# Arithmetic on SBUF moved from Pool to VectorE and TensorE, and a 64x64 product moved from the norms to the third feed-forward pair

## The chip, the cores and the metric

The kernel runs on one core of one Trainium2 chip. The metric is the device time of one launch in microseconds (us); smaller is better. The engines of a core go by the names of the profile: PE is TensorE's matmul, PEld its weight load, DVE is VectorE, ACT is ScalarE, POOL is GpSimd (Pool in the text), SP is SyncE, which issues the loads of the weights.

## What is computed

Two layers of a decoder trunk on 256 tokens of width 1024, in float32. The reference, cut to its skeleton:

```python
h = x
for i in range(2):
    xn = rmsnorm(h, norm_mix[i])
    u_nsa, u_hgrn, u_ret, u_rwkv = split(xn @ w_in[i])
    outs = nsa(u_nsa), hgrn2(u_hgrn), retention(u_ret), rwkv7(u_rwkv)      # 256 wide each
    merged = sum(sigmoid(xn @ w_gate[i, m] + b_gate[i, m]) * (outs[m] @ w_branch[i, m]) for m in range(4))
    h = h + merged @ w_out[i]
    hn = rmsnorm(h, norm_ffn[i])
    h = h + (silu(hn @ w_ffn_gate[i]) * (hn @ w_ffn_up[i])) @ w_ffn_down[i]   # 2816 wide
    hp = rmsnorm(h, norm_ple[i])
    h = h + sigmoid(hp @ w_ple_gate[i]) * (p[i] @ w_ple_proj[i])
return rmsnorm(h, norm_final)
```

rmsnorm divides each token by the root of the mean of its 1024 squares (plus 1e-6) and multiplies by a gain per feature.

## The kernel before

Activations lie feature-major, [128 features, 8 chunks, 256 tokens], so that weights are TensorE's stationary operand and tokens the moving one. A GEMM keeps float32 accuracy by splitting both operands in a high and a low part. `w_load` (lines 197 to 213) takes a weight tile of 128x1024: SP's queue loads it (512 KB) into `wr`, ACT copies it into the high part `wh` (L211), and a subtraction gives the low part `wl` (L212); there are 4 buffers of `wr` and 3 each of `wh` and `wl`. `mm3` (L226 to L228) then issues three matmuls per block of 128x128, wl with xh, wh with xl, wh with xh, each over 256 columns: 24 matmuls per tile. `gemm_pair` (L261 to L263) is the same for two output chunks, with the last contraction chunks put last where these are produced late.

The subtraction goes to DVE or to Pool: Pool takes every fourth tile (`wcount % 4 == 3`) while `shared` is set, which is from the gates of the mixer m=3 on to the next layer, and at the last stage of a layer a list, `lo_plan`, names the engine tile by tile. Pool also adds the merged branches (L1255), multiplies in the feed-forward stage (L1343), adds up squares for the norms (L336, L340, L345) and does one residual add per layer (L1365, by `adders`).

A layer goes through these stages: input projection and the four mixers; the gates and branches of the mixers, m = 2, 1, 3, 0; the projection w_pp of p; w_out with a residual; 11 pairs of feed-forward chunks (two gate tiles and two up tiles each); w_fd with a residual; and the PLE stage, which is four pairs of w_pg, a tanh, a product and the add to h (L1362 to L1365). The order of the instructions on each engine is made by a scheduler from priorities; `issue_after` pins one instruction behind another.

A norm is spread: `h_done` is called for each finished chunk of h, makes its high and low parts (L315, L316), squares it (L327, L331) and adds squares up. `h_stat` (L348 to L372) sums the squares over features by products with a column of 1/1024 (L354, 128x1, two per accumulated tile), takes the root in ten small DVE operations (L285 to L299), and spreads it over the partitions with two matmuls (L359). The GEMMs that follow don't wait for it: their results are multiplied by it afterwards. Where `steady` is set (at the first norm, behind both w_out, and between the layers), a product of 64x64 with two columns, whose result nobody reads, follows the spreading:

```python
with self.tc.issue_after(bcast.ins):
    q = slice(0, 64)
    self.nc.tensor.matmul(bc[q, T:T + 2], self.ident[q, q], self.ident[q, :2], start=True, stop=True,
                          tile_position=(0, 0), skip_group_check=True)
```

This product (L365) is called the quarter product here. Four of them run, one for each norm that `steady` names.

## Time and profile before

| quantity | value |
|---|---|
| time, median of 3 runs | 1037.78 us (1036.01 to 1038.59) |
| time of the profiled execution | 1037.06 us |
| span of the profiled execution | 1035.3 us |
| mean granted clock of TensorE | 0.994 |
| PE busy | 1016.1 us, 98% |
| DVE busy | 735.6 us, 71% |
| ACT busy | 542.1 us, 52% |
| POOL busy | 241.9 us, 23% |

The span is what the trace covers; 1.8 us of the profiled execution's own time lie around it. The profile gives TensorE's granted clock in shares of its full speed of 2.4 GHz; 0.5 is its lower level, 1.2 GHz. The shares are averages over stages. A wait in the trace is put down to the semaphore that came last. Matmuls overlap, so the pace of a stream of matmuls is read from their starts: each lasts 0.28 us, and the next starts long before it ends.

### The profile page before, as it was taken

How to read it: one execution, taken by the hardware profiler on the slowest of the kernel's cores; microseconds unless marked ns; L12 is line 12 of the kernel's file. 1: busy time of each engine (PE TensorE's matmuls, PEld its weight loads, DVE VectorE, ACT ScalarE, POOL GpSimd, SP SyncE). 2: the span in 40 equal slices, each digit the busy share in tenths (PEclk: the TensorE clock that was granted, in tenths of full speed). 3: DMA queues.
4: the chain of work that ended last, by engine and by line, in shares of the span. 5: the costliest groups of instructions: out<-in, count | busy, mean ns of one | idle time of the engine just before them, and what ended most of it. 6: DMA issues, size and time to landing. Idle time of an engine off the chain costs nothing.

```text
span 1035.3 us, 22817 instructions
## 1 busy us (share of the span) xinstructions
PE 1016.1 (98%) x9528; PEld 975.6 (94%) x9528; DVE 735.6 (71%) x1216; ACT 542.1 (52%) x863; POOL 241.9 (23%) x154
## 2 busy tenths in 40 slices
PE   9999999999999999999899999999999999999996
PEld 8999988899999999999898999988999999999995
DVE  6899968766676767554877999577556767765556
ACT  5644555554664555454545545556546555454444
POOL 0100000054442233233410000000544333242322
PEclk9999999999999999999999999999999999999998
DMA  8565233255665666666544553333656665666651
GB/s 292 183 201 157 90 104 109 76 163 175 208 198 167 204 200 185 194 187 206 167 156 128 182 165 103 103 103 102 173 185 183 193 189 179 207 191 192 182 185 53
DMA packets 50503, 171.33 MB, mean 165 GB/s; under 512 B 5856, under 2 KB 6624, under 8 KB 50272
## 3 DMA queue, kind: packets, MB, share of 16 engines
q1 hardware_dynamic: 50112, 169.76, 53.4%
q8 instruction: 75, 1.23, 0.5%
q14 instruction: 28, 0.23, 0.1%
q10 hardware_dynamic: 288, 0.11, 0.0%
HBM read 168.80 MB, written 1.05 MB: 164 GB/s over the span
## 4 chain that ended last, share of the span: by engine, by line
PE 86%; DVE 9%; ACT 2%; issue 1%; DMA 1%; POOL 1%; DVEq 0%; ACTq 0%; POOLq 0%
PE mm L226 21%; PE mm L227 21%; PE mm L228 21%; PE pB L141 6%; PE pA L141 5%; DVE wl L212 2%; PE pA L226 2%; PE pA L227 2%; PE pA L228 2%; PE pA L261 1%; PE pA L262 1%; PE pA L263 1%; ACT wh L211 1%; DVE T L1364 1%; PE mm L438 1%
## 5 line engine op out<-in xcount | busy, mean ns | idle before, releaser
L211 ACT ACTIVATE wh<-wr 128x1024 fp32r<-128x1024 f32 (+3 forms) x314 | 325.4, 1040 | 333.8 <-PE mm L228 221.2
L212 DVE TENSOR_TENSOR wl<-wr,wh 128x1024 fp32r<-128x1024 f32 (+3 forms) x259 | 325.2, 1257 | 131.7 <-ACT wh L211 130.6
L226 PE MATMUL mm<-xh,wl 128*128 128x256 f32 x1472 | 412.6, 280 | 1.4 <-POOL wl L212 1.4
L228 PE MATMUL mm<-xh,wh 128*128 128x256 f32 x1472 | 411.1, 279 | 0.0
L227 PE MATMUL mm<-xl,wh 128*128 128x256 f32 x1472 | 411.0, 279 | 0.0
L226 PEld LDWEIGHTS mm<-xh,wl 128*128 128x128 f32 x1472 | 276.7, 188 | 5.3 <-POOL wl L212 1.8
L227 PEld LDWEIGHTS mm<-xl,wh 128*128 128x128 f32 x1472 | 277.1, 188 | 3.0 <-issue 1.4
L228 PEld LDWEIGHTS mm<-xh,wh 128*128 128x128 f32 x1472 | 276.7, 188 | 2.5 <-issue 1.1
L212 POOL TENSOR_TENSOR wl<-wr,wh 128x1024 fp32r<-128x1024 f32 (+1 forms) x55 | 130.3, 2370 | 260.8 <-ACT wh L211 260.8
L226 PE MATMUL mm<-A,wl 128*128 128x256 f32 x332 | 91.6, 276 | 0.0
L227 PE MATMUL mm<-A,wh 128*128 128x256 f32 x332 | 91.6, 276 | 0.0
L228 PE MATMUL mm<-A,wh 128*128 128x256 f32 x332 | 91.6, 276 | 0.0
L1343 POOL TENSOR_TENSOR B<-B,B 128x512 f32<-128x512 f32 x22 | 28.4, 1292 | 145.7 <-DVE B L1341 139.4
L226 PEld LDWEIGHTS mm<-A,wl 128*128 128x128 f32 x332 | 62.3, 188 | 0.0
L227 PEld LDWEIGHTS mm<-A,wh 128*128 128x128 f32 x332 | 62.3, 188 | 0.0
L228 PEld LDWEIGHTS mm<-A,wh 128*128 128x128 f32 x332 | 62.3, 188 | 0.0
L382 DVE TENSOR_TENSOR A<-B,A 128x512 fp32r<-128x512 f32 x18 | 36.8, 2042 | 33.2 <-ACT A L381 33.2
L141 PE MATMUL pA<-A,A 64*64 64x64 f32 (+3 forms) x1008 | 49.7, 223 | 1.2 <-DVE A L644 1.2
L141 PEld LDWEIGHTS pA<-A,A 64*64 64x64 f32 (+3 forms) x1008 | 41.6, 135 | 9.0 <-DVE A L644 1.6
L1255 POOL TENSOR_TENSOR M<-M,T 128x512 f32<-128x512 f32 x24 | 43.4, 1843 | 9.9 <-DVE T L1254 9.9
L226 PE MATMUL mm<-Y,wl 128*128 128x256 f32 x160 | 44.8, 280 | 0.0
L227 PE MATMUL mm<-Y,wh 128*128 128x256 f32 x160 | 44.5, 278 | 0.0
(393 smaller groups left out, 1741.9 us busy)
## 6 DMA issues: line engine op xcount, KB each, us to landing
wr<-in_w_gate_dram SPq DMA_DIRECT2D x64, 512.0 KB, 3.7
wr<-in_w_fm_dram SPq DMA_DIRECT2D x46, 512.0 KB, 3.7
wr<-in_w_fg_dram SPq DMA_DIRECT2D x44, 512.0 KB, 4.6
wr<-in_w_fu_dram SPq DMA_DIRECT2D x44, 512.0 KB, 3.7
wr<-in_w_fd_dram SPq DMA_DIRECT2D x32, 512.0 KB, 4.2
wr<-in_w_branch_dram SPq DMA_DIRECT2D x16, 512.0 KB, 4.2
wr<-in_w_out_dram SPq DMA_DIRECT2D x16, 512.0 KB, 3.8
wr<-in_w_pg_dram SPq DMA_DIRECT2D x16, 512.0 KB, 3.9
```

The costliest lines, as they stand in the source:

```text
L141: f(*args, **kw)
L211: nc.scalar.activation(hi[:, s], raw[:, s], AF.Copy)
L212: e.tensor_sub(lo[:, s], raw[:, s], hi[:, s])
L226: mm(out, wlo, xhi, start=start, stop=False)
L227: mm(out, whi, xlo, start=False, stop=False)
L228: mm(out, whi, xhi, start=False, stop=stop)
L261: mm(ps[:, c], lo, xs[k][0], start=c == 0 and k == 0, stop=False, skip_group_check=True)
L262: mm(ps[:, c], hi, xs[k][1], start=False, stop=False, skip_group_check=True)
L263: mm(ps[:, c], hi, xs[k][0], start=False, stop=k == n - 1, skip_group_check=True)
L382: self.nc.vector.tensor_sub(lo, src, hi)
L1255: self.nc.gpsimd.tensor_add(merged[p], merged[p], ths[p])
L1343: G.tensor_mul(up, th, up)
```

## The change

All of Pool's arithmetic on SBUF goes to DVE: the subtraction of 55 weight tiles, 22 products of the feed-forward stage, 24 adds of merged branches, the adds of squares and two residual adds. Pool keeps memsets, conversions and small copies. At the PLE stage `h_done` is called with `plain`: there, only the squares of the first two chunk pairs are added (on DVE), and the others go to TensorE as they are, so that six tiles instead of two (layer 0) or four (layer 1) are multiplied with the column of 1/1024. The quarter products behind the norms are gone; in each layer one stands before the gate product of the third feed-forward pair, pinned behind the matmul that was issued last.

```diff
--- before.py
+++ after.py
@@ -201,15 +201,11 @@
         raw = self.wp.tile([P, 1024], F32, tag="wr", name=f"wr{self.n}", bufs=WRAW)
         hi = self.wp.tile([P, 1024], F32R, tag="wh", name=f"wh{self.n}", bufs=WSPL)
         lo = self.wp.tile([P, 1024], F32R, tag="wl", name=f"wl{self.n}", bufs=WSPL)
-        self.wcount += 1
-        e = nc.gpsimd if self.wcount % 4 == 3 and self.shared else nc.vector
-        if self.lo_plan:
-            e = nc.gpsimd if self.lo_plan.pop(0) == "P" else nc.vector
         for i in range(0, n, n // parts):
             s = slice(i, i + n // parts)
             self.last_load = nc.sync.dma_start(raw[:, s], src[:, s])
             nc.scalar.activation(hi[:, s], raw[:, s], AF.Copy)
-            e.tensor_sub(lo[:, s], raw[:, s], hi[:, s])
+            nc.vector.tensor_sub(lo[:, s], raw[:, s], hi[:, s])
         return hi, lo
 
     def w_tiles(self, src, parts=1):
@@ -225,7 +221,14 @@
         mm = self.nc.tensor.matmul
         mm(out, wlo, xhi, start=start, stop=False)
         mm(out, whi, xlo, start=False, stop=False)
-        mm(out, whi, xhi, start=False, stop=stop)
+        self.last_mm = mm(out, whi, xhi, start=False, stop=stop)
+
+    def quarter(self, ps):
+
+        q = slice(0, 64)
+        with self.tc.issue_after(self.last_mm.ins):
+            self.nc.tensor.matmul(ps[q, 0, :2], self.ident[q, q], self.ident[q, :2], start=True, stop=True,
+                                  tile_position=(0, 0), skip_group_check=True)
 
     def mm2(self, out, w, x, start, stop):
 
@@ -300,7 +303,7 @@
         return y
 
 
-    def h_done(self, ch, gcol, tag=None, first=False, part=None):
+    def h_done(self, ch, gcol, tag=None, first=False, part=None, plain=False):
 
         nc = self.nc
         p, c = divmod(ch, 2)
@@ -329,9 +332,16 @@
                 return
         else:
             nc.scalar.activation(sq, self.h[:, ch - 1:ch + 1], AF.Square)
-        add = nc.vector.tensor_add if first else nc.gpsimd.tensor_add
+        add = nc.vector.tensor_add
         if p == 0:
             self.acc = sq
+        elif plain and p > 1:
+
+            if p == 2:
+                self.accs = [self.acc[:, 0], self.acc[:, 1]]
+            if p == 2 or c == 1:
+                self.accs += [sq[:, 0], sq[:, 1]]
+            return
         elif p < 3 - (gcol is None):
             add(self.acc, self.acc, sq)
         if p == 2:
@@ -345,7 +355,7 @@
                 add(sq[:, 0], sq[:, 0], sq[:, 1])
                 self.accs.pop()
 
-    def h_stat(self, last=False, steady=False):
+    def h_stat(self, last=False):
         nc = self.nc
         ps = self.ps([P, 512], "pB")
         n = len(self.accs)
@@ -356,14 +366,8 @@
         self.rt = self.rsqrt(ps[:, 0:2], 2, 1.0, EPS)
         bc = self.ps([P, 512], "pB")
         for tc_ in range(2):
-            bcast = nc.tensor.matmul(bc[:, tc_ * P:(tc_ + 1) * P], self.rt[:, tc_:tc_ + 1].to_broadcast([P, P]), self.ident,
+            nc.tensor.matmul(bc[:, tc_ * P:(tc_ + 1) * P], self.rt[:, tc_:tc_ + 1].to_broadcast([P, P]), self.ident,
                              start=True, stop=True)
-        if steady:
-
-            with self.tc.issue_after(bcast.ins):
-                q = slice(0, 64)
-                self.nc.tensor.matmul(bc[q, T:T + 2], self.ident[q, q], self.ident[q, :2], start=True, stop=True,
-                                      tile_position=(0, 0), skip_group_check=True)
         self.rstd_ps = bc[:, None, :T].to_broadcast([P, 2, T])
         if last:
             return
...
@@ -1191,14 +1195,9 @@
         self.omlb = [om[:, 2 * l:2 * l + 2] for l in range(L)]
 
     def body(self):
-        self.wcount = 0
-
-        self.shared = False
         self.tc.cur_priority += Front.AHEAD
         self.xp = [None] * 4
         self.stream = "B"
-
-        self.lo_plan = list("VVVVV")
         self.setup()
         for p in range(4):
             for c in range(2):
@@ -1206,7 +1205,7 @@
             if p == 2:
                 self.ahead.append(self.w_tiles([self.ins["w_fm"][0, 7]], 2))
                 self.nc.sync.dma_start(self.h[:, 6:8], self.ins["x"][:, 6:8])
-        self.h_stat(steady=True)
+        self.h_stat()
         for l in range(L):
             self.layer(l)
 
@@ -1252,18 +1251,17 @@
                     V.scalar_tensor_tensor(merged[p], ths[p], 1.0, ps, op0=OP.add, op1=OP.mult)
                 else:
                     V.scalar_tensor_tensor(ths[p], ths[p], 1.0, ps, op0=OP.add, op1=OP.mult)
-                    self.nc.gpsimd.tensor_add(merged[p], merged[p], ths[p])
+                    V.tensor_add(merged[p], merged[p], ths[p])
 
     def layer(self, l):
         nc = self.nc
-        V, G = nc.vector, nc.gpsimd
+        V = nc.vector
         ins = self.ins
         v = lambda col: self.vec[l][:, col:col + 1]
         vh = lambda col: self.vech[l][:, col:col + 1]
         self.merged = [None] * 4
         lane = self.lane
         self.lanes = dict.fromkeys("GAB", self.tc.cur_priority)
-        self.shared = False
         with lane("G"):
             ums = self.rwkv_in(l)
         with lane("A", "G"):
@@ -1302,7 +1300,6 @@
         with lane("G"):
             self.tc.cur_priority += (200, 100)[l]
             for m, y in ((2, y2), (1, y1), (3, y3), (0, y0)):
-                self.shared = m in (3, 0)
                 self.branch(l, m, self.gates(l, m), y)
         self.tc.cur_priority = max(self.lanes.values())
 
@@ -1330,6 +1327,8 @@
         xs = []
         for p in range(NF // 2):
             pg = self.ps([P, 2, T], "mm" if p else "pA")
+            if p == 2:
+                self.quarter(pg)
             self.gemm_pair(pg, [[ins["w_fg"][l, 2 * p + c]] for c in range(2)], self.xs(), 0 if p else 2)
             pu = self.ps([P, 2, T], "mm" if p else "pA")
             self.gemm_pair(pu, [[ins["w_fu"][l, 2 * p + c]] for c in range(2)], self.xs())
@@ -1340,15 +1339,13 @@
             up = self.g([P, 2, T])
             V.tensor_mul(up, pu, self.rstd_b)
             V.scalar_tensor_tensor(th, th, 1.0, a, op0=OP.add, op1=OP.mult)
-            G.tensor_mul(up, th, up)
+            V.tensor_mul(up, th, up)
             xs += self.split(up, "A" if p < 9 else "T")
         self.residual(lambda c: [ins["w_fd"][l, c, :, a:min(a + 1024, DFF)] for a in range(0, DFF, 1024)], xs,
                       lambda c: self.vec[l][:, V_PLE + c:V_PLE + c + 1], ("U", "U", "U", "M"))
 
         xs = self.xs()
         gcol = (lambda c: self.vec[l + 1][:, V_MIX + c:V_MIX + c + 1]) if l + 1 < L else None
-        self.lo_plan = list(("VVVPPPVVVP", "VVVVVVPVVPVVVP")[l])
-        adders = ("PVVV", "VPVV")[l]
         for p in range(4):
             parts = self.pair([[ins["w_pg"][l, 2 * p + c]] for c in range(2)], xs, 0 if p else 2,
                               "mm" if p > 1 else "pA", p == 3)
@@ -1362,10 +1359,10 @@
                     V.tensor_mul(dc, ps[:, :, ts], self.rstd[:, None, ts].to_broadcast([P, n, ts.stop - ts.start]))
                     nc.scalar.activation(dc, dc, AF.Tanh, scale=0.5)
                     V.scalar_tensor_tensor(dc, dc, 1.0, pps[p][:, c:c + n, ts], op0=OP.add, op1=OP.mult)
-                    (G if adders[p] == "P" else V).tensor_add(hc, dc, hc)
+                    V.tensor_add(hc, dc, hc)
                     for i in range(n):
-                        self.h_done(2 * p + c + i, gcol, part=ts if len(halves) > 1 else None)
-        self.h_stat(l + 1 == L, l + 1 < L)
+                        self.h_done(2 * p + c + i, gcol, part=ts if len(halves) > 1 else None, plain=True)
+        self.h_stat(l + 1 == L)
 
     def residual(self, src, xs, gcol, tag=None):
 
@@ -1377,7 +1374,7 @@
                 V.scalar_tensor_tensor(hc, ps, 0.5, hc, op0=OP.mult, op1=OP.add)
                 for i in range(n):
                     self.h_done(2 * p + c + i, gcol, tag)
-        self.h_stat(steady=tag is None)
+        self.h_stat()
```

How the instructions move is shown at three places, by the programs' own numbers of tiles and buffers.

On PE, at the norm behind w_out in layer 0, the program before spreads the root (L359) and issues the quarter product between two matmuls of the first up tile (mm_503 is the sum of the first pair's up product, wh504 and wl504 its first weight tile):

```order
L228 MATMUL mm_503_4293<-xh_173,wh504_4295 128x256
L359 MATMUL pB_490_4153<-cst_155,rs_y2B_489_4142 128x128 x2
L365 MATMUL pB_490_4153<-cst_155 64x2
L226 MATMUL mm_503_4293<-xh_173,wl504_4296 128x256
L227 MATMUL mm_503_4293<-xl_174,wh504_4295 128x256
```

The changed program there:

```order
L224 MATMUL mm_503_4291<-xh_173,wh504_4293 128x256
L222 MATMUL mm_503_4291<-xh_173,wl504_4294 128x256
L369 MATMUL pB_490_4152<-cst_155,rs_y2B_489_4141 128x128 x2
L223 MATMUL mm_503_4291<-xl_174,wh504_4293 128x256
L224 MATMUL mm_503_4291<-xh_173,wh504_4293 128x256
```

Further on, 90 rows behind that L369, stands the third pair (mm_514 is the sum of its gate product, mm_506 that of the second pair's up product):

```order
L223 MATMUL mm_506_4352<-xl_174,wh508_4384 128x256
L224 MATMUL mm_506_4352<-xh_173,wh508_4384 128x256
L230 MATMUL mm_514_4425<-cst_155 64x2
L222 MATMUL mm_514_4425<-xh_173,wl515_4429 128x256
L223 MATMUL mm_514_4425<-xl_174,wh515_4428 128x256
```

Behind the norm the quarter product is gone, and between the second and the third pair, in an unbroken stream of matmuls, there is one.

On DVE, at the PLE stage of layer 0, the program before has these rows from the last pair's first split to the add of h of the third pair (T_675 is the third pair's product, T_681 the fourth's, wl680 the last split of w_pg, wl693 the first of the next layer's input projection, xl_174 the low parts of h):

```order
L212 TENSOR_TENSOR wl680_6630<-wr680_6628,wh680_6629 128x1024
L316 SCALAR_TENSOR_TENSOR xl_174<-h_156,vec1_158,xh_173 128x256 x2
L1362 TENSOR_TENSOR T_675_6583<-mm_672_6522,rstd_661_6375 128x512
L316 SCALAR_TENSOR_TENSOR xl_174<-h_156,vec1_158,xh_173 128x256 x2
L212 TENSOR_TENSOR wl693_6705<-wr693_6703,wh693_6704 128x1024
L1364 SCALAR_TENSOR_TENSOR T_675_6583<-T_675_6583,Y3_456_3821 128x512
L1362 TENSOR_TENSOR T_681_6658<-mm_677_6596,rstd_661_6375 128x256
L1365 TENSOR_TENSOR h_156<-T_675_6583,h_156 128x512
```

The changed program, from the first split of the input projection on:

```order
L208 TENSOR_TENSOR wl693_6708<-wr693_6706,wh693_6707 128x1024
L1361 SCALAR_TENSOR_TENSOR T_675_6582<-T_675_6582,Y3_456_3820 128x512
L1359 TENSOR_TENSOR T_681_6655<-mm_677_6593,rstd_661_6374 128x256
L208 TENSOR_TENSOR wl694_6714<-wr694_6712,wh694_6713 128x1024
L319 SCALAR_TENSOR_TENSOR xl_174<-h_156,vec1_158,xh_173 128x256 x2
L1362 TENSOR_TENSOR h_156<-T_675_6582,h_156 128x512
L346 TENSOR_TENSOR B_666_6446<-B_666_6446,B_671_6518 128x512
L1359 TENSOR_TENSOR T_681_6655<-pA_679_6624,rstd_661_6374 128x256
L208 TENSOR_TENSOR wl698_6776<-wr698_6774,wh698_6775 128x1024
```

The split of tile 694 and the add of squares, which were Pool's, stand in DVE's queue, the split ahead of the add of h.

On PE, in the first input projection of layer 1 (pA_692, tiles 693 and 694; pA_697 with tile 698 is the next), the sums of squares (pB_683) stand so before:

```order
L261 MATMUL pA_692_6702<-xh_173,wl693_6705 128x256
L354 MATMUL pB_683_6675<-inv_dm_76,B_666_6447 128x1 x2
L226 MATMUL pA_697_6770<-xh_173,wl698_6773 128x256
L227 MATMUL pA_697_6770<-xl_174,wh698_6772 128x256
L228 MATMUL pA_697_6770<-xh_173,wh698_6772 128x256
```

and so in the changed program:

```order
L264 MATMUL pA_692_6705<-xh_173,wl693_6708 128x256
L364 MATMUL pB_683_6671<-inv_dm_76,B_666_6446 128x1 x4
L364 MATMUL pB_683_6671<-inv_dm_76,B_676_6591 128x1 x4
L222 MATMUL pA_697_6773<-xh_173,wl698_6776 128x256
L223 MATMUL pA_697_6773<-xl_174,wh698_6775 128x256
```

Eight products take the place of two. A second group follows further on, of two products before and of four now.

## Rows read from the trace of the kernel before

**Rows 1.** The page's first part: busy us and share of the span, xinstructions, per engine

```profile
PE 1016.1 (98%) x9528; PEld 975.6 (94%) x9528; DVE 735.6 (71%) x1216; ACT 542.1 (52%) x863; POOL 241.9 (23%) x154
```

**Rows 2.** Waits of PE: engine line waited for: us in total, times, longest us

```profile
PE pB L359 <- DVE rs_y2B L299: 2.5, 2, 1.9
PE pA L261 <- ACT xh L315: 1.9, 1, 1.9
PE mm L226 <- POOL wl L212: 1.4, 2, 0.7
```

**Rows 3.** Timeline of POOL: start us, us, line, out<-in xcount [idle before <-releaser]

```profile
495.86 7.09 POOL L212 TENSOR_TENSOR wl<-wr,wh 128x1024 fp32r<-128x1024 f32 x3 [4.14 <-ACT wh L211]
...
511.56 2.88 POOL L212 TENSOR_TENSOR wl<-wr,wh 128x1024 fp32r<-128x1024 f32 x1 [1.19 <-ACT wh L211]
```

**Rows 4.** Timeline of DVE in the PLE stage of layer 0

```profile
495.97 2.29 DVE L299 SCALAR_TENSOR_TENSOR rs_y2B<-rs_u2B,rs_z2B 128x2 f32<-128x2 f32 x1
...
505.88 0.68 DVE L1364 SCALAR_TENSOR_TENSOR T<-T,Y 128x512 f32<-128x512 f32 x1
...
512.11 2.89 DVE L1364 SCALAR_TENSOR_TENSOR T<-T,Y 128x512 f32<-128x512 f32 x1
```

**Rows 5.** Groups by line and shape: xcount | busy us, mean ns | idle before

```profile
L212 DVE TENSOR_TENSOR wl<-wr,wh 128x1024 fp32r<-128x1024 f32 x235 | 301.0, 1282 | 121.2 <-ACT wh L211 120.2
L212 POOL TENSOR_TENSOR wl<-wr,wh 128x1024 fp32r<-128x1024 f32 x51 | 122.9, 2411 | 247.1 <-ACT wh L211 247.1
L1255 POOL TENSOR_TENSOR M<-M,T 128x512 f32<-128x512 f32 x24 | 43.4, 1843 | 9.9 <-DVE T L1254 9.9
L1343 POOL TENSOR_TENSOR B<-B,B 128x512 f32<-128x512 f32 x22 | 28.4, 1292 | 145.7 <-DVE B L1341 139.4 <-DVE B L1342 6.3
```

**Rows 6.** Windows: us, busy (xcount) of PE, PEld, DVE, ACT, POOL; clock, DMA, GB/s

```profile
25.00:39.00 14.00, 14.00 (x121) 14.00 (x120) 13.94 (x37) 9.55 (x17) 1.67 (x2) 1.00 0.75 259
323.00:343.00 20.00, 20.00 (x179) 20.00 (x178) 14.98 (x16) 10.65 (x13) 5.88 (x4) 1.00 0.63 191
766.00:796.00 30.00, 30.00 (x256) 30.00 (x256) 20.48 (x21) 17.53 (x27) 12.34 (x6) 1.00 0.63 193
517.60:521.20 3.60, 3.60 (x19) 3.60 (x19) 2.95 (x5) 1.75 (x4) 2.86 (x2) 0.53 0.26 25
```

**Rows 7.** Timeline of PE at a norm with, and one without, the quarter product

```profile
320.84 0.60 PE L359 MATMUL pB<-cst,rs_y2B 128*128 128x128 f32 x4
...
321.80 0.28 PE L227 MATMUL mm<-xl,wh 128*128 128x256 f32 x1
...
1011.13 0.61 PE L359 MATMUL pB<-cst,rs_y2B 128*128 128x128 f32 x4
...
1011.69 0.28 PE L226 MATMUL mm<-U,wl 128*128 128x256 f32 x1
```

**Rows 8.** Timeline of PE around two L354 products (four passes, from 313.10)

```profile
312.98 0.28 PE L226 MATMUL pA<-xh,wl 128*128 128x256 f32 x1
...
313.66 0.28 PE L228 MATMUL pA<-xh,wh 128*128 128x256 f32 x1
```

**Rows 9.** Timeline of PE, first input projection of layer 1

```profile
514.29 0.28 PE L263 MATMUL pA<-xh,wh 128*128 128x256 f32 x1
516.52 0.39 PE L261 MATMUL pA<-xh,wl 128*128 128x256 f32 x1 [1.95 <-ACT xh L315]
517.38 0.39 PE L262 MATMUL pA<-xl,wh 128*128 128x256 f32 x1 [0.47 <-DVE xl L316]
...
528.19 0.39 PE L226 MATMUL pA<-xh,wl 128*128 128x256 f32 x1 [1.17 <-DVE wl L212]
```

**Rows 10.** Timeline of DVE at the end of layer 1

```profile
1015.96 2.32 DVE L212 TENSOR_TENSOR wl<-wr,wh 128x1024 fp32r<-128x1024 f32 x1
...
1023.64 0.48 DVE L1362 TENSOR_TENSOR T<-pA,rstd 128x128 f32<-128x128 f32 x2
```

**Rows 11.** Timeline of PE: the last matmul of layer 1's GEMMs

```profile
1021.78 0.28 PE L228 MATMUL pA<-M,wh 128*128 128x256 f32 x1
```

More of the change, by code (lines that the diff above doesn't have):

```diff
@@ L1254, in branch @@
                     V.scalar_tensor_tensor(ths[p], ths[p], 1.0, ps, op0=OP.add, op1=OP.mult)
-                    self.nc.gpsimd.tensor_add(merged[p], merged[p], ths[p])
+                    V.tensor_add(merged[p], merged[p], ths[p])
     def layer(self, l):
         nc = self.nc
-        V, G = nc.vector, nc.gpsimd
+        V = nc.vector
         ins = self.ins
```

## The prediction

> **What bounds the kernel now.** I read the page's first part, then the waits of PE, then pieces of the timelines at those waits, then windows over unbroken streams of matmuls. PE is busy 98% of the span, DVE 71% and POOL 23% [rows 1], and PE's whole list of waits that matter to this change is short [rows 2]: 2.5 us at the spreading of the norm's root, 1.9 on one high part of h, 1.4 on splits made by POOL. So the kernel is bound by PE, and a change that only moves work off POOL can't give more than the few places where PE stands still or runs below its pace. Three things are to be seen there.
>
> First, POOL in the way of DVE. At 495.97 the last of the small operations of the root took DVE 2.29 us for 128x2 elements, and at 512.11 an operation on 128x512 took 2.89 us where the same line took 0.68 at 505.88 [rows 4]. POOL was in a split of a weight tile both times [rows 3]. Then PE waited: 514.29 to 516.52 for a high part of h, to 517.38 for its low part, and later, before 528.19, for a split of DVE [rows 9]. Directly behind the first two the granted clock was 0.53, near the lower of its two levels: 19 matmuls in 3.6 us [rows 6].
>
> Second, two paces at full clock. In a window the count holds all that overlap it, so the pace is the window plus 0.28 us, divided by the count: 118 ns at 25 to 39 and at 766 to 796, 113 ns at 323 to 343, each at granted clock 1.00 with PE never idle [rows 6]. The difference is 5 ns a matmul. What sets the pace is not shown by any counter; it changes where the stream is broken. In layer 0's feed-forward stage it is fast from the quarter product on.
>
> Third, the quarter product costs time itself: from the first pass of the spreading to the second matmul behind it 0.96 us with it (320.84 to 321.80) and 0.56 without (1011.13 to 1011.69) [rows 7], so 0.40 us each.
>
> **The change, part by part**, against the profiled execution's 1037.06 us, which is 0.72 below the median of the runs.
>
> *POOL's splits before the gates' matmuls.* Two waits of PE, 1.4 us [rows 2], end, as a DVE split is done in 1.28 us on the mean where POOL needs 2.41 [rows 5]. The second stops at 765.8, and the matmuls behind it run slowly for 30 us: 256 at 118 ns [rows 6]. Without the break I take them at 113: 256 x 5 ns = 1.3. Sum -2.7; bounds 0 (the splits are late on DVE as well, and the pace stays) and -2.7.
>
> *DVE's load.* It takes on 55 splits at 1.28 us or less, 22 products and 24 adds [rows 5] at 0.68 (the undisturbed row of that size [rows 4]) and the small adds that I put at 10 us: 70 + 15 + 16 + 10 = 111 us. With nothing saved it would be busy 847 us, 82%; as the lengthened rows shorten, I expect 765 to 800. In the feed-forward stage a pair is 96 matmuls x 113 ns = 10.85 us of PE, and DVE then has 4 splits (5.1) and five operations of 0.68 (3.4): 8.5 us. In the gate stage, per mixer, 240 matmuls are 27.1 us, against 10 splits (12.8) and twelve of 0.68 (8.2): 21.0. So these edits cost nothing there, covered by the matmuls; were they not covered, each uncovered split would cost PE up to 1.3 us. SP's queue keeps its loads and their order.
>
> *The quarter products.* Four go and two come: -2 x 0.40 = -0.8. Bounds -0.4 and -1.2, if one in an unbroken stream, which no row of before shows, costs half or one and a half times as much.
>
> *The pace around the norms.* Without a quarter product behind w_out's norm, the 90 matmuls up to the third pair may stay slow: 90 x 5 ns = 0.45 per layer, +0.9. At the first norm and between the layers the stream behind the quarter product was slow (121 matmuls from 25 to 39 [rows 6]); were two such stretches fast, they would give 2 x 121 x 5 ns = -1.2. I take 0 and keep both ends. From the third pair on I take the fast pace as before.
>
> *The PLE stage of layer 0 and the next input projection.* The rows of waits there hold 2.23 - 0.11 = 2.1 us (514.29 to 516.52), 0.5 (before 517.38), 1.2 (before 528.19) [rows 9], and the half clock 3.6 - 19 x 0.113 = 1.45 [rows 6]: 5.25 in all, which comes back if DVE brings the third pair of h in time. DVE's queue from the end of the root to that add of h is, by the changed order, five splits (5 x 1.28 = 6.4 [rows 5]) and, in operations of 512 columns, two and a half products with the root, three at L1361, three adds and four low parts of half the size, 10.5 x 0.68 = 7.1 [rows 4]: 13.5 us. The root ended at 495.97 + 2.29 = 498.3 [rows 4], and PE wanted that part of h at 514.3, 16.0 us later. The margin is 2.5 us, less the copy of the high part on ACT and the gaps between operations. So the wait on h goes, barely. The wait at the spreading itself, 2.5 - 1.9 = 0.6 [rows 2], stays about as it is: the 2.29 us fall to a tenth, but two splits that were POOL's now stand between the small operations. Against it stand the sums of squares: 16 more passes of the column product in layer 0. Four such passes cost 313.66 - 312.98 less two matmuls, 0.68 - 0.23 = 0.45 us [rows 8], 0.11 each, 1.8 in all. And since these products now wait for DVE's last add of squares and ACT's squares, with matmuls of tile 698 queued behind, I leave 0.8 for new waits. Sum -5.25 + 1.8 + 0.8 = -2.6; bounds -4.0 (no new waits, and 0.6 of the spreading's wait gone as well) and +1.8 (all waits stay). Layer 1's 8 additional passes lie where PE is idle: nothing.
>
> The Trainium skill (TensorEngine Tiling (Array Packing), Performance Considerations, Instruction Overhead) puts the fixed cost of a matmul at about 60 cycles, whatever its few columns. At the full clock that is an estimate of 25 ns a pass and 0.4 us for the 16, where the sum has 1.8; the row of this trace shows more, and it decides.
>
> *The tail.* The last matmul of a GEMM starts at 1021.78 [rows 11], lasting to about 1022.1, but DVE multiplies its result only at 1023.64, some 1.5 us later, since its queue was held up from 1015.96 on by a split of 2.32 us [rows 10]. Undisturbed it is done in 1.28. I take -1.5; bounds 0 and -1.9, the largest wait of the tail [rows 2].
>
> Sum: -2.7 - 0.8 + 0 - 2.6 - 1.5 = -7.6, so 1029.5 by the profiled execution and 1030.2 for the median.
>
> **The rivals.** (1) *The quarter product in the stream sets the slow pace, or leaves it.* It stands behind an unbroken stream, where no quarter product stood before; of the four before, two were followed by matmuls at 118 ns (25 to 39 is one) and two by matmuls at 113 (323 to 343) [rows 6]. From it to the PLE stage there are nine pairs of 96 and 8 x 66 of w_fd, 1392 matmuls a layer: 1392 x 5 ns = 7.0 us. In both layers: 1030.2 + 13.9 = 1044.1, slower than before. Where 1500 of these 2784 go at 118 ns, the gain of 7.6 us is undone; with some 2150 it is slower by 0.3%. In one layer alone: 1037.2. For it: half of the four; against it: both quarter products of the feed-forward stage were followed by the fast pace.
>
> The Trainium skill (TensorE: Matmul & The Clock Gate, "Wait — 56ns, not 53.3ns?") gives warm matmuls one pace, columns at 2.4 GHz plus about 2.5 ns, an estimate of 109 ns for 256 columns. By that, this rival could not happen, and the terms of pace would be nothing. The trace has 118 and 113 at the same granted clock [rows 6], so I don't exclude it.
>
> (2) *DVE becomes the bound of the PLE stage.* The margin of 2.5 us is thin. If it fails, the waits and the half clock stay, the additional passes are paid (+1.8 for -2.6), and the tail gives nothing: -2.7 - 0.8 + 1.8 = -1.7, 1036.1. For it: DVE's queue has no pause there. Against it: the row of 2.89 us turns into 0.68, and that of 2.29 shrinks too [rows 4].
>
> (3) *POOL's work was hidden anyway*: PE's waits pass to DVE's splits, and what is left is the quarter products, -0.8: 1037.0.
>
> **How the numbers follow.** Forecast 0.55, rival 1 in both layers 0.15 and in one 0.08, rival 2 0.16, rival 3 0.06. A measurement tells 0.3%, about 3.1 us: faster is below 1034.7, slower above 1040.9. The forecast's own bounds, its terms taken at their better ends (-2.7, -1.2, -1.2, -4.0, -1.9 make -11.0, not all at once) and some at their worse, give 1027 to 1035. Faster: nearly all of the forecast, and half of rival 2, if only a part of the waits stays: 0.63. Same: rivals 3, the one layer of rival 1 and the rest of 2: 0.21. Slower: rival 1 and a little of the others: 0.16. The range reaches to rivals 2 and 3 and the one layer, and leaves out rival 1 in both: 1026.5 to 1038.
>
> **What would show it.** Right: POOL gone from PE's waits and busy some 10 us; L1361 at 0.68 us each; about 179 matmuls per 20 us through the feed-forward stage; no half clock at the first input projection of layer 1; DVE below 80%. Wrong: some 171 matmuls per 20 us behind the quarter product (rival 1), or a wait of 2 us on a high part of h near 515 with the low clock behind it (rival 2).

## The result and the profile after

| | kernel before | changed kernel |
|---|---|---|
| median | 1038.36 us (8 runs, 1036.01 to 1039.33) | 1032.37 us (8 runs, 1029.01 to 1034.91) |
| profiled execution, span | 1037.06, 1035.3 us | 1034.50, 1032.7 us |

The ratio is 0.9945, 95% interval 0.9932 to 0.9957: 5.7 us less, between 4.5 and 7.1. The forecast was 7.6 less. The changed kernel was run again later beside other kernels and took 1031.24 us (ratio 0.9936, 0.9922 to 0.9949). Its runs scatter more than those of before, and the scatter goes with the mean granted clock: 1029.01 at 0.996, 1034.91 at 0.993.

The page's first part, in the columns of [rows 1]:

```profile
PE 1016.8 (98%) x9548; PEld 976.8 (95%) x9548; DVE 770.4 (75%) x1337; ACT 541.1 (52%) x863; POOL 7.6 (1%) x28
```

POOL's 242 us are down to 7.6, and DVE gained only 35, though 46 operations of 0.68 us and 55 splits came to it: its own grew shorter. The groups by line and shape, as in [rows 5]:

```profile
L208 DVE TENSOR_TENSOR wl<-wr,wh 128x1024 fp32r<-128x1024 f32 x286 | 349.2, 1222 | 138.7 <-ACT wh L207 137.0
L1254 DVE TENSOR_TENSOR M<-M,T 128x512 f32<-128x512 f32 x24 | 15.4, 681 | 0.0
L1342 DVE TENSOR_TENSOR B<-B,B 128x512 f32<-128x512 f32 x22 | 15.2, 692 | 0.7
L1361 DVE SCALAR_TENSOR_TENSOR T<-T,Y 128x512 f32<-128x512 f32 x6 | 4.1, 688 | 0.3
```

A split takes 1.22 us where the mean was 1.28, and the product of the last stage 0.69, without the rows of 2.89 us [rows 4].

The waits of PE, as in [rows 2]:

```profile
PE mm L141 <- DMA T<-in_w_cmp_dram: 1.9, 2, 1.0
PE pB L369 <- DVE rs_y2B L302: 1.9, 1, 1.9
PE pA L264 <- DVE wl L208: 1.5, 2, 0.8
...
PE pA L264 <- ACT xh L318: 0.6, 1, 0.6
```

The waits for POOL are gone, that for the high part of h fell from 1.9 to 0.6, and one is new: a load of w_cmp, in the mixers of each layer. PE's larger waits for splits of DVE were 1.9 us before (1.2 and 0.7) and are 1.9 now (1.5 and 0.4), so the waits for POOL did not pass to them.

Both kernels have 7104 matmuls of the GEMMs in the trace (a triple, below, is the three that `mm3` issues for one block). Where the n-th of them starts shows where the time went. The comparison uses the later profile of the changed kernel (1031.06 us, near its median) against that of before (1037.06), 6.0 us in all:

| stretch, to GEMM matmul | before | changed | gained in it |
|---|---|---|---|
| start and mixers of layer 0, 1320 | 252.65 | 253.84 | -1.2 |
| rest of the gates and branches, 1640 | 290.82 | 290.50 | 1.5 |
| w_out to the third feed-forward pair, 1990 | 332.70 | 332.42 | 0.0 |
| feed-forward stage and w_fd, 3350 | 487.43 | 486.56 | 0.6 |
| last stage, next input projection, 3780 | 547.30 | 543.90 | 2.5 |
| mixers of layer 1, 4860 | 760.83 | 758.44 | -1.0 |
| rest of the gates and branches, 5190 | 800.77 | 796.26 | 2.1 |
| to the last one, 7103 | 1021.78 | 1017.26 | 0.0 |
| from there to the last matmul of the tail | | | 1.5 |

The changed kernel's first profile is 3.4 us longer. It differs from this one above all in three rows: the start and the mixers of layer 0 lose 1.8 us there, the last stage gains only 0.9, with the clock at its lower level for 6.9 us against 3.4, and the stretch to the last matmul loses 0.9. At the start of that last stretch the same matmuls in the same order, at full clock and with nothing waiting, go at 118 ns in the first profile and at 113 in the later one (columns as in [rows 6], the first profile, then the later one):

```profile
796.20:816.20 20.00, 20.00 (x172) 20.00 (x171) 15.35 (x22) 12.98 (x19) 0.00 (x0) 1.00 0.63 192
```

```profile
793.70:813.70 20.00, 20.00 (x178) 20.00 (x178) 15.81 (x23) 13.67 (x21) 0.00 (x0) 1.00 0.67 196
```

So the order of a program does not settle the pace alone.

### The profile page after: what moved, and what is told of

Same layout as the page of the kernel before. It is cut to its first block, busy times and chain, and to the rows that moved or that the text cites. A ratio compares the mean times of both kernels' runs of the same rounds, so it can differ in the third digit from the quotient of the medians.

```text
span 1032.7 us, 22828 instructions
## 1 busy us (share of the span) xinstructions
PE 1016.8 (98%) x9548; PEld 976.8 (95%) x9548; DVE 770.4 (75%) x1337; ACT 541.1 (52%) x863; POOL 7.6 (1%) x28
## 4 chain that ended last, share of the span: by engine, by line
PE 88%; DVE 7%; DMA 2%; issue 2%; ACT 1%; SPq 0%; DVEq 0%; ACTq 0%
PE mm L222 22%; PE mm L223 21%; PE mm L224 21%; PE pB L141 6%; PE pA L141 5%; DVE wl L208 2%; PE pA L222 2%; PE pA L223 2%; PE pA L224 2%; DMA T<-in_w_cmp_dram 1%; PE pA L264 1%; PE pA L265 1%; PE pA L266 1%; DMA cst<-in_consts_dram 1%; PE pB L364 1%
## 5 line engine op out<-in xcount | busy, mean ns | idle before, releaser
L208 DVE TENSOR_TENSOR wl<-wr,wh 128x1024 fp32r<-128x1024 f32 (+3 forms) x314 | 375.0, 1196 | 143.2 <-ACT wh L207 141.4
L223 PE MATMUL mm<-Y,wh 128*128 128x256 f32 x160 | 44.4, 277 | 0.0
L224 PE MATMUL mm<-Y,wh 128*128 128x256 f32 x160 | 44.2, 276 | 0.0
L1230 DVE TENSOR_TENSOR T<-mm,rstd 128x512 f32<-128x512 f32 x32 | 22.1, 689 | 13.9 <-PE mm L224 13.9
L1233 ACT ACTIVATE T<-T,vech 128x256 f32<-128x256 f32 x64 | 28.8, 500 | 2.6 <-DVE T L1230 2.6
L222 PEld LDWEIGHTS mm<-Y,wl 128*128 128x128 f32 x160 | 30.1, 188 | 0.0
```

Of the source, the lines that this page charges most:

```text
L208: nc.vector.tensor_sub(lo[:, s], raw[:, s], hi[:, s])
L222: mm(out, wlo, xhi, start=start, stop=False)
L223: mm(out, whi, xlo, start=False, stop=False)
L224: self.last_mm = mm(out, whi, xhi, start=False, stop=stop)
L1230: self.nc.vector.tensor_mul(th, ps, self.rstd_b)
L1233: self.nc.scalar.activation(th[:, c], th[:, c], AF.Tanh, scale=0.5, bias=self.vech[l][:, col:col + 1])
```

## The experiments

Every kernel here computes the whole reference; the last of the twelve is the changed kernel once more. Medians stand with the ratio to the kernel before, which ran beside them. In the diffs, lines that begin with a minus are the changed kernel's, if nothing else is said.

### The quarter product in the feed-forward stage

No quarter product at all:

```diff
-            if p == 2:
-                self.quarter(pg)
```

> The changed kernel without the two quarter products of the feed-forward stage. Theory A, the quarter product brings the stream from 118 to 113 ns a matmul: without it the 87 matmuls at 118 ns that stand behind the spreading of the norm go on to the end of w_fd, about 1390 more matmuls a layer x 5 ns x 2 = 13.9 us, less 0.8 for the two products: about 1045 us against 1032.4 for the changed kernel. Rival B, the pace comes back by itself at the next tile or pair: 1031.5 us, 0.8 less than the changed kernel, and 113 ns in the windows of the feed-forward stage.

Measured: 1044.16 us (5 runs, 1043.88 to 1046.04), 1.0057 (1.0045 to 1.0069). The windows from 331 to 351 us, of the changed kernel and then of this one (columns as in [rows 6]):

```profile
331.00:351.00 20.00, 20.00 (x179) 20.00 (x178) 14.35 (x18) 10.19 (x12) 0.00 (x0) 1.00 0.62 188
```

```profile
331.00:351.00 20.00, 20.00 (x172) 20.00 (x172) 14.06 (x17) 9.74 (x11) 0.00 (x0) 1.00 0.65 185
```

172 matmuls against 179, so 118 ns against 113 (20.28 us by the count), with the same clock and nothing waiting. Theory A holds: without the product the change would have made the kernel 6 us slower instead of faster.

The quarter products behind the norms, as before, and none in the stage (in `h_stat`, at the four norms that had it):

```diff
+            with self.tc.issue_after(self.last_mm.ins):
+                self.nc.tensor.matmul(bc[q, T:T + 2], self.ident[q, q], self.ident[q, :2], start=True, stop=True,
+                                      tile_position=(0, 0), skip_group_check=True)
...
-                self.quarter(pg)
```

> The changed kernel with the four quarter products behind the norms, as before, and none in the feed-forward stage; Pool's work stays on DVE and TensorE. Theory A, the gain of the change is Pool's work, and the move of the quarter products is worth little: two more of 0.4 us and slow stretches behind the first norm and between the layers (2 x 113 x 5 ns = 1.1) cost 1.9, the 87 matmuls a layer that are then at 113 ns give back 0.9: about 1033.4. Rival B, the move of the quarter products carries most of the 6 us: 1036 or more.

Measured: 1037.06 us, 0.9994 (0.9969 to 1.0020), with 12 runs from 1030.25 to 1044.90. The median lies where rival B put it; the scatter of 15 us neither theory foresaw. The profiled execution (1041.06) had both feed-forward stages at 118 ns, as in the window above; the lowest times leave no room for that. So with Pool's work on DVE a quarter product behind the norm seems to bring the pace of 113 ns in some executions and not in others; that is argued from the times, as no short execution of this kernel was profiled. The runs of the kernel before lie within 4 us, which leaves no room for a stage that loses 7. The orders differ at that place: before, the spreading and the quarter product stood between two triples of matmuls [rows 7]; here, the same rows stand behind the first matmul of a triple.

That led to the next one: the product in the stage, but one matmul later, inside a triple.

```diff
-        mm(out, wlo, xhi, start=start, stop=False)
+        first = mm(out, wlo, xhi, start=start, stop=False)
+        if self.hook is not None and start:
+            self.last_mm = first
+            self.quarter(self.hook)
```

> The changed kernel with the quarter product of the feed-forward stage one matmul later, behind the first of a triple of matmuls and not between two triples (it writes another PSUM buffer, which nobody reads). Theory A, what counts is that it stands between two triples: inside one it leaves the stream at 118 ns, in each execution or in some of them, and the runs scatter between 1031 and 1045 as with the quarter products behind the norms, median over 1035. Rival B, what counts is that it stands in an unbroken stream: 1032.4 us and 113 ns, as in the changed kernel.

Measured: 1030.95 us (1030.60 to 1032.93), 0.9934 (0.9922 to 0.9946). Rival B holds: in an unbroken stream the place in the triple doesn't matter.

A quarter product one pair earlier (from the kernel with two parts undone, below):

```diff
-            if p == 2:
+            if p == 1:
                 self.quarter(pg)
```

> The same with the quarter product before the second instead of the third feed-forward pair. Theory A, the 118 ns stretch behind the norm is cut from 87 to about 41 matmuls a layer: 2 x 46 x 5 ns = 0.5 us less, at the edge of what can be told, and 113 ns behind it. Rival B, so near to the norm it leaves the pace at 118 ns in some executions: runs 7 us longer.

Measured: 1044.47 us (1042.47 to 1045.61), 1.0062 (1.0049 to 1.0074). Both theories misplaced it. PE's timeline:

```profile
318.25 0.27 PE L230 MATMUL mm<-cst 64*64 64x2 f32 x2
318.45 0.39 PE L222 MATMUL mm<-xh,wl 128*128 128x256 f32 x1
...
319.15 0.60 PE L369 MATMUL pB<-cst,rs_y2B 128*128 128x128 f32 x4
319.51 0.36 PE L224 MATMUL mm<-xh,wh 128*128 128x256 f32 x1
```

The spreading of the root comes behind the quarter product, five GEMM matmuls on, and the rest of the stage goes at 118 ns. (The norm lies in the second pair; where the part on the change calls mm_503 the first pair's up product, it is the second pair's gate product.) That fits the last break before a long stream deciding its pace. In the 14 profiles (both kernels and the twelve runs), 18 quarter products stood in a stream with no spreading behind them, and behind all 18 the stream went at 113 ns.

### The move of the quarter products alone

From the kernel before, with Pool's work left as it was:

```diff
-        self.h_stat(steady=tag is None)
+        self.h_stat()
...
+            if p == 2:
+                self.quarter(pg)
```

> The kernel before with the move of the quarter products alone: none behind the norms, one before the third feed-forward pair; Pool keeps its work. Theory A, the move is worth little here, since behind both w_out the quarter product of before stands between two triples of matmuls and brings 113 ns already: two products fewer (-0.8), 2 x 87 matmuls at 118 ns more (+0.9), two stretches of some 115 matmuls behind the first norm and between the layers at 113 instead of 118 (-1.1, if they come out so): 1037 against 1038. Rival B, the move carries most of the gain also without Pool's part: 1033 to 1034.

Measured: 1039.28 us (12 runs, 1037.28 to 1041.36), 1.0016 (1.0007 to 1.0024). The move alone makes the kernel 1.7 us slower. Its trace is that of its shortest execution (1037.28), so it need not show all of this. Against that of before: 0.35 us gained up to GEMM matmul 288, 0.5 behind by matmul 480, so some 0.9 lost within the mixers of layer 0; and in each layer 73 matmuls at 118 ns between w_out's norm and the third pair, where before all but the first few go at 113. The spreading stands between two triples there in both kernels: with the quarter product behind it 113 ns follow, without it 118. The move is needed, then, as far as these runs show, only because the move of Pool's work takes the pace behind the norm away.

### Pool's work, part by part

Every fourth split of m = 3 and 0 back on Pool, ten in all, and with them the 24 adds of merged branches:

```diff
-            nc.vector.tensor_sub(lo[:, s], raw[:, s], hi[:, s])
+            e.tensor_sub(lo[:, s], raw[:, s], hi[:, s])     # e: gpsimd if wcount % 4 == 3 and shared
...
-                    V.tensor_add(merged[p], merged[p], ths[p])
+                    self.nc.gpsimd.tensor_add(merged[p], merged[p], ths[p])
```

> The changed kernel with every fourth split back on Pool in the gates and branches of m = 3 and 0, in both layers. Theory A, these splits are what stopped PE: about 0.9 us of waiting per layer comes back, and in layer 1 the break again leaves some 250 matmuls at 118 ns (1.3 us): 1034 to 1035.5 us. Rival B, the gain of that stage came from the adds on Pool, which held these splits up, and without the adds Pool is in time: 1032.4 us, no wait on a split of Pool.

Measured: 1032.39 us (6 runs, 1030.44 to 1035.98), 0.9939 (0.9923 to 0.9955). The profiled execution was the longest, 1035.98, and shows what theory A said; the waits of PE and a window behind the second:

```profile
PE mm L224 <- POOL wl L210: 1.4, 2, 0.7
```

```profile
766.00:810.00 44.00, 44.00 (x376) 44.00 (x376) 31.84 (x36) 25.91 (x37) 9.87 (x5) 1.00 0.63 199
```

The wait is there and 118 ns behind it ((44 + 0.28) / 376). But the median is that of the changed kernel: in other executions the pace must have come out otherwise. And the pace does not belong to the wait: the kernel with the move of the quarter products alone, and the one with the last stage alone (below), have the same two waits, 1.4 us, and 113 ns behind both. The latter, in layer 1:

```profile
764.60:784.60 20.00, 20.00 (x179) 20.00 (x178) 11.21 (x14) 10.65 (x15) 5.09 (x3) 1.00 0.68 211
```

So the trace shows 1.4 us of waiting for these splits, and whatever the pace behind the break makes of it; against the changed kernel's median it can't be told from nothing. Rival B is not tested, since the adds, which it wants on DVE, went back to Pool as well.

The merged adds and the products back on Pool:

```diff
-                    V.tensor_add(merged[p], merged[p], ths[p])
+                    self.nc.gpsimd.tensor_add(merged[p], merged[p], ths[p])
...
-            V.tensor_mul(up, th, up)
+            nc.gpsimd.tensor_mul(up, th, up)
```

> The changed kernel with the 24 adds of merged branches and the 22 products of the feed-forward stage back on Pool. Theory A, these moves cost and give nothing, as DVE has room beside the matmuls there and no wait of PE hangs on them: 1032.4 us, PE's waits as in the changed kernel. Rival B, Pool's two-input operations lengthen DVE's splits in the gate stage so that PE waits for them, or make the high parts late: 1034 us or more, with waits of PE for a split of DVE in the gate stage.

Measured: 1029.74 us (4 runs, 1028.74 to 1030.22), 0.9917 (0.9904 to 0.9930). Rival B falls, and the time lies below theory A's too: these moves gain nothing.

The sums of squares of layer 0's last stage on DVE:

```diff
-                        self.h_done(2 * p + c + i, gcol, part=..., plain=True)
+                        self.h_done(2 * p + c + i, gcol, part=..., plain=l + 1 == L)
```

> The changed kernel with the sums of squares of layer 0's last stage added on DVE again, so that 4 products with the column stand there instead of 12. Theory A, the sixteen passes in one block that hardly work the array are what brings (or prolongs) the low clock from 516 to 522 us and cost about 1.5 us themselves: the low clock goes or is half as long, 1029 to 1030.5 us. Rival B, the waits for h ahead of them bring the low clock and DVE's adds make these longer by up to 1.1 us: the low clock stays as long, 1032.5 to 1034 us.

Measured: 1030.75 us (1029.19 to 1031.85), 0.9921 (0.9909 to 0.9933). The changed kernel's PE at that place, and this one's:

```profile
514.44 0.38 PE L264 MATMUL pA<-xh,wl 128*128 128x256 f32 x1 [0.64 <-ACT xh L318]
514.66 2.25 PE L364 MATMUL pB<-inv_dm,B 128*128 128x1 f32 x16
516.77 0.56 PE L222 MATMUL pA<-xh,wl 128*128 128x256 f32 x1
```

```profile
514.04 0.38 PE L264 MATMUL pA<-xh,wl 128*128 128x256 f32 x1 [0.65 <-ACT xh L318]
515.66 0.36 PE L222 MATMUL pA<-xh,wl 128*128 128x256 f32 x1 [1.23 <-DVE wl L208]
```

The time lies just above theory A's range. The block of 16 passes takes 2.1 us here, where the clock falls within it, and 1.7 in the changed kernel's later profile. But it also covers a wait of 1.2 for a split that DVE brings no sooner without it: of its price 0.7 is left (2.33 us from the first row to the last, against 1.62), by the later profile 0.3 (1.92). What theory A said of the clock can't be held. Between 500 and 560 us it was at its lower level for 26 GEMM matmuls in the changed kernel's first profile, for 16 in its later one, and for 16 in this kernel; in four of the 14 profiles, with 16-pass blocks and without, it was never.

Both undone together (this and the merged adds and products):

> The changed kernel with two parts undone that the other runs showed to cost: layer 0's sums of squares of the last stage on DVE (4 products with the column instead of 12), and the 24 merged adds and 22 products back on Pool. Theory A, both gains are there together as they lie in different stages: 1.6 and some 2 us, so 1028 to 1029.5. Rival B, they are the same scatter (low clock, pace) read twice: 1029.7 to 1031.

> The changed kernel itself, on the same chip as the three others, as their comparison: 1032.4 us if its first runs stand for it. Should it come out at 1030, the 2 us by which the kernels with the sums on DVE and with the adds on Pool were below it are scatter of its runs.

Measured: 1030.65 us (1029.70 to 1031.82), 0.9931 (0.9919 to 0.9943), and the changed kernel beside it 1031.24 (1029.90 to 1032.16), 0.9936 (0.9922 to 0.9949). The two gains don't add up; rival B holds. That one of the parts costs up to 2 us isn't shown; they are worth nothing that these runs can tell, and no kernel here beats the changed one clearly.

The last stage of both layers as before:

```diff
+        self.lo_plan = list(("VVVPPPVVVP", "VVVVVVPVVPVVVP")[l])
+        adders = ("PVVV", "VPVV")[l]
...
-        add = nc.vector.tensor_add
+        add = nc.gpsimd.tensor_add if pool else nc.vector.tensor_add
```

> The changed kernel with the last stage of both layers as before: some splits, one add of h a layer and the sums of squares on Pool, 4 and 8 products with the column instead of 12 and 12. Theory A, DVE alone is quicker there, above all at the end of layer 1: the tail's 1.5 us come back, and against the kernel with only the sums on DVE (1030.75) it loses 2.5 to 3: 1033 to 1034. Rival B, the last stage is bound by DVE's queue as much as by Pool's, and the moves there are worth nothing: 1030 to 1031.5.

Measured: 1039.44 us (11 runs, 1037.86 to 1040.24), 1.0012 (1.0003 to 1.0021). Theory A's sign, at about three times its size (8.7 us against 1030.75), and by another way than it said. The timelines of POOL and of DVE, and a wait of PE:

```profile
495.31 7.01 POOL L209 TENSOR_TENSOR wl<-wr,wh 128x1024 fp32r<-128x1024 f32 x3 [280.18 <-ACT wh L208]
```

```profile
495.17 0.16 DVE L297 TENSOR_TENSOR rs_u2B<-rs_u2B,rs_i2B 128x2 f32<-128x2 f32 x1
495.37 2.36 DVE L298 SCALAR_TENSOR_TENSOR rs_z2B<-rs_u2B,rs_i2B 128x2 f32<-128x2 f32 x1
497.76 2.27 DVE L299 SCALAR_TENSOR_TENSOR rs_u2B<-rs_z2B,rs_x2B 128x2 f32<-128x2 f32 x1
500.07 2.26 DVE L300 TENSOR_TENSOR rs_u2B<-rs_u2B,rs_z2B 128x2 f32<-128x2 f32 x1
502.37 0.17 DVE L301 TENSOR_SCALAR rs_z2B<-rs_z2B 128x2 f32<-128x2 f32 x1
```

```profile
PE pB L370 <- DVE rs_y2B L303: 7.0, 2, 5.1
```

Three of the root's small operations wait, each for one split of POOL. Before, one did [rows 4], since POOL's splits began 1.5 us behind the chain's first operation there and begin 0.7 behind it here (494.58). PE waits 5.1 us for the root, and the clock is at its lower level from 501.5 to 508.4. By these two traces, how much Pool's work costs in this stage hangs on a few tenths of a microsecond.

And the last stage alone, from the kernel before:

```diff
-        self.lo_plan = list(("VVVPPPVVVP", "VVVVVVPVVPVVVP")[l])
-        adders = ("PVVV", "VPVV")[l]
+        self.shared = False
...
-        add = nc.vector.tensor_add if first else nc.gpsimd.tensor_add
+        add = nc.vector.tensor_add if first or plain else nc.gpsimd.tensor_add
```

> The kernel before with the last stage of both layers alone as in the change: no split, no add of h and no sum of squares on Pool there, 12 products with the column in each layer. Pool keeps the splits of the gates and the feed-forward stage, the merged adds and the products; the quarter products stay behind the norms. Theory A, this stage carries the gain, the rest of the change being worth 1 to 2 us together: 1033 to 1034.5 against 1037.8. Rival B, the gain is spread, or the pace of the feed-forward stage is lost when the norm before it is not followed by the same place in the stream: 1036 to 1038, or runs that scatter by 7 us.

Measured: 1034.46 us (1032.69 to 1035.61), 0.9962 (0.9950 to 0.9975): 3.9 us less, in theory A's range. It is the largest part of the gain.

## Why the prediction was right

The time lay in the range, and the sign and the likeliest case were right. That the sum is so near is in part luck: the gates gave 0.9 us more than it had, the mixers took 2.2 that it did not have, and the last stage came near its term by a working that was wrong. By its steps:

- *Pool's splits before the gates' matmuls*, -2.7: the two stretches gained 1.5 and 2.1 us between the aligned traces. The waits ended as said, 1.4 us. The term of pace, 1.3, was read from one execution and is not a loss that these waits always bring: before had 113 ns behind the first wait and 118 behind the second, and two other kernels with the same waits had 113 behind both.
- *DVE's load*, nothing: right, busy 770.4 us where 765 to 800 was expected, and no wait in the feed-forward stage.
- *The quarter products*, -0.8: the price of one in the stream, which no row of before showed, is what was taken. From the matmul ahead of it to the third one behind it are 0.76 us, where three at 118 ns take 0.35:

```profile
330.01 0.28 PE L224 MATMUL mm<-xh,wh 128*128 128x256 f32 x1
330.22 0.27 PE L230 MATMUL mm<-cst 64*64 64x2 f32 x2
...
330.77 0.28 PE L224 MATMUL mm<-xh,wh 128*128 128x256 f32 x1
```

- *The pace around the norms*, 0: right as a sum. The stretch behind w_out's norm stayed at 118 ns, as the worse end had it (87 matmuls, some 0.4 us a layer); between the layers it came out at 113 in the profiles of the changed kernel. Rival 1 fell by all 18 quarter products; but the kernel with none took the time that rival 1 forecast, 1044.1.
- *The last stage and the next input projection*, -2.6: 2.5 us came by the later profile, 0.9 by the first. The working was wrong in two places. (The 16 more passes cost 1.7 at full clock, near its 1.8.) "So the wait on h goes, barely" failed: 0.6 us of it stayed, and the low clock behind it. The window, columns as in [rows 6], and the timelines of DVE and of PE show why:

```profile
516.70:522.30 5.60, 5.60 (x27) 5.60 (x28) 2.32 (x6) 1.52 (x4) 0.00 (x0) 0.50 0.29 94
```

```profile
495.27 1.22 DVE L208 TENSOR_TENSOR wl<-wr,wh 128x1024 fp32r<-128x1024 f32 x1
496.42 0.15 DVE L296 TENSOR_TENSOR rs_u2B<-rs_u2B,rs_i2B 128x2 f32<-128x2 f32 x1
496.49 1.22 DVE L208 TENSOR_TENSOR wl<-wr,wh 128x1024 fp32r<-128x1024 f32 x1
...
498.47 0.16 DVE L302 SCALAR_TENSOR_TENSOR rs_y2B<-rs_u2B,rs_z2B 128x2 f32<-128x2 f32 x1
...
501.57 1.22 DVE L208 TENSOR_TENSOR wl<-wr,wh 128x1024 fp32r<-128x1024 f32 x1 [1.49 <-ACT wh L207]
502.72 1.28 DVE L1359 TENSOR_TENSOR T<-pA,rstd 128x512 f32<-128x512 f32 x2
```

```profile
501.08 0.60 PE L369 MATMUL pB<-cst,rs_y2B 128*128 128x128 f32 x4
```

The root ends at 498.6, but PE issues the spreading at 501.1, where the scheduler put it in PE's queue: 2.8 us later than before. PE's wait there is gone. DVE stands idle for 1.5 us ahead of the split at 501.57, and its products of the last stage, behind that split, start at 502.7. The margin of 2.5 us went into that idle time, the copy of the high part on ACT (0.5), and PE, which comes to that place 0.8 us sooner than before (513.8 against 514.6).

- *The tail*, -1.5: 1.5 in both profiles. DVE reads the last product 0.3 us behind the last matmul's start, where it was 1.9 [rows 10, 11]:

```profile
1021.01 0.49 DVE L1359 TENSOR_TENSOR T<-pA,rstd 128x128 f32<-128x128 f32 x2 [0.41 <-PE pA L224]
```

- *A term that was missing*: the mixers, 2.2 us lost in both layers together. The sum gave 7.6, and 5.7 came. In each layer PE now waits for a load of w_cmp, at most 1.0 us in the first profile and 0.8 in the later one, where SP issues it no earlier than before (68.2 us against 68.3 in layer 0), and PE's order there has moved. In layer 0 this comes with the quarter products (the kernel with their move alone loses 0.9 there, the one with the last stage alone nothing between matmuls 288 and 480); what sets it off in layer 1 is open.

## What to carry to other kernels

Read the order of the changed program at every wait that a sum counts on, and on both engines: a wait that ends on one can come back as a later place in the other's queue. Where an unbroken stream of matmuls has two paces, find what stood last before it: here one product of 0.4 us, in the right place, was worth 7 us a layer, and a change that moves instructions can lose it without a wait to show for it. Try the parts of a change both ways, alone and left out: the quarter product's move costs 1.7 us alone, and without it the rest gives nothing certain. And see a pace in more than one execution before it goes into a sum: the 1.3 us behind POOL's second wait were read from one, and two other kernels with the same wait don't have them.

## What was not expected of the hardware

The pace behind a break follows a pattern only in part. In the 14 profiles a spreading (four passes of 128x128) with no quarter product directly behind it was followed by 118 ns 50 times out of 52 where the second matmul of a triple came next, but 8 times out of 14 where a triple began next, and twice out of six where the third matmul came next. With a quarter product directly behind it, it was followed by 113 ns six times out of six where a triple began next, and by 118 five times out of six where the second of a triple came next. And one order of matmuls had both paces in two executions (172 and 178 in 20 us, above). What the engine does at such a place isn't shown by any row.

A DVE operation on 128x2 elements takes 0.16 us, but 2.3 to 2.4 where it starts just behind a split of POOL, all five times that this happened in the profiles. A chain of ten of them took 1.8 us at its shortest and 8.2 at its longest.
